# A second-layer transformer trunk kernel: one more product of the feed-forward stage as a pair, and operands of the group computed ahead emitted later

## The chip, the cores and the metric

The kernel runs on one core of a Trainium2 chip. The metric is the device time of one execution in microseconds (us); the number given for a kernel is the median of several runs. The profiles come from one further execution each, whose own time differs a little from the median.

## The reference

Two layers of a hybrid block on 512 positions of width 1024, all in 32-bit floats. A layer has a branch of matrix memory (mLSTM), a branch of retention, their gated merge, a feed-forward step and a gated embedding. The change is in the feed-forward step alone; in the reference it is two lines:

```python
h2 = rmsnorm(x, norm2_g[i])
x = x + jnp.square(jax.nn.relu(h2 @ w_ff1[i] + b_ff1[i])) @ w_ff2[i] + b_ff2[i]
```

`w_ff1[i]` is 1024 by 4096 and `w_ff2[i]` 4096 by 1024.

## The kernel before

**Products.** Activations lie transposed: 128 partitions of a feature tile by 512 positions. Each 32-bit factor is split in a high and a low part that TensorE takes at full rate: ACT copies the high part (L326), VectorE subtracts it from the source for the low part (L327). A product is then three matmuls: high by high, high by low, low by high. There are two forms for a group of two output tiles:

- two **T8** units (`t8`, matmuls at L518 to L520): per unit one weight tile of 128 by 1024 and 24 matmuls of 512 columns;
- one **PAIR** unit (`run_pair`, matmuls at L573 to L575): a scheme of Strassen and Winograd with seven products P1, P5, P6, P2, P3, P7, P4 of 12 matmuls of 256 columns each. P4 is put off: it is kept in `later` and issued by `flush`, behind P5 of the next unit (or in the middle of the next T8).

A pair takes its weights in the pieces A (for P1, P5), B (P6, P2), C (P3, P7), each 128 by 1024, and D (P4), 128 by 512. Half of each of A, B and C, and all of D, are sums of weight blocks (`t1` to `t4`). POOL makes them ahead in DRAM with accumulating DMAs (`step`, L384), one at a time, paced by a credit that grows with each unit by a share of its time: `SHARE`, and `LATER` from some unit on. Each step also waits for the matmul that was the last one issued when it was written. SP loads the pieces (`fill_raws`) into four raw buffers; three buffers hold split pieces A, B and C (and whole tiles of T8), one holds D. So a split piece waits on ACT until an older piece has been used, and a low part on VectorE for its high part on ACT.

**The feed-forward stage.** The 4096 inner features are four groups b of four parts p. `f(b,p)` computes a part of the first product with `ff1` and keeps it as an operand of the second; `o(b,p)` is a pair of the second product, adding group b's share to two tiles of x with `ff2`. The order is written out in `ff_order`: f(0,0) to f(0,3); then for b = 0, 1, 2: f(b+1,0), o(b,0) to o(b,3), f(b+1,1) to f(b+1,3); then o(3,0) to o(3,3). So f(b+1,0) is computed ahead, before group b is added up. `FPAIRS` lists for each layer which (b,p) of the first product are pairs; the others are two T8.

In `ff1`, `evac` takes each half out of PSUM: VectorE multiplies by the norm's factor (L1535), ACT does relu (L1536) and the square (L1537). From the result `st` two helpers make the operand that a pair needs, in seven quarters of 256 columns: `pair_quarters` splits the first three (a 768-column split on ACT and VectorE), and `pair_operand` forms the four inner ones on VectorE (L668, L669, L670) and splits them (a 1024-column split). The parts are `hid[b, p]`, in the trace `l0hh` and `l0hl` (or `l1hh`, `l1hl`), with five buffers each; `st` has two buffers (`l0f20st` is that of f(2,0) in layer 0).

In `ff2` each of the seven products is added onto x by VectorE as soon as it is done: L1573, or L1571 the first time, when the bias is added too. The products share three PSUM banks per pair, named in the trace by a letter behind the unit's name (`l1o11a` is bank a of o(1,1) in layer 1): P1, P6, P7 and P4 use a, P5 and P3 use c, and P2 uses b. P2 adds onto a copy of P1 that ACT puts into b (L579). So P7 can only begin when P6 has been added to x, and P3 when P5 has. Evictions are given a higher priority (`ahead`) in the scheduler that settles the order of each engine's queue; each engine then works through its queue in that order, and a row that waits holds up all behind it.

Of the kernel before, what the change touches and what calls it, by code (L numbers as in the profile page):

```python
# [87 lines left out]

FPAIRS = (((1, 1), (1, 3), (2, 1), (2, 3), (3, 1)), ((0, 2), (1, 0), (1, 1), (1, 3), (2, 0), (2, 1), (2, 3), (3, 0), (3, 1), (3, 2)))


PRODUCTS = {"P1": ("A", 0, 0), "P5": ("A", 1, 4), "P2": ("B", 0, 2), "P6": ("B", 1, 5), "P3": ("C", 0, 6),
# [14 lines left out]
HALVES = [(WIDE[x][0], u) for x, u in TURNS]  # L109

SOON = ("w_in", 0, CGM + 2 * P)
STEP, SHARE, LATER = 1.13, 0.75, 0.75
TIME = {"PAIR": (9.9, 3.9), "WIDE": (5.45, 2.7), "FULL": (9.9, 5.0)}


# [37 lines left out]
def groups():  # L153
# [3 lines left out]
    for i in range(L):  # L157
# [11 lines left out]
        for b in range(4):  # L169
            f = [p for c, p in FPAIRS[i] if c == b]  # L170
            if f:
# [5 lines left out]
def unit_list(i):  # L177
# [10 lines left out]
    def pair(g, p):  # L188
        u.append(("PAIR", (i, g), p))
# [51 lines left out]
    def pairs(seq):  # L241
        for kind, b, p in seq:
            if (b, p) in FPAIRS[i] and kind == "f":
                pair(f"fp{b}", [q for c, q in FPAIRS[i] if c == b].index(p))
            elif kind == "f":
# [13 lines left out]
def build(ctx, tc, ins, out):  # L259
# [65 lines left out]
    def split(src, hi_ap, lo_ap):  # L325
        a = ac.activation(hi_ap, src, AF.Copy)  # L326
        return a, ve.tensor_sub(lo_ap, src, hi_ap.bitcast(F32))  # L327
# [194 lines left out]
    def t8(act, name):  # L522

        _, wh, wl = unit("T8")
        o = ps(name)
        for k in range(KT):
            s = slice(k * P, (k + 1) * P)
            mm3(o, wh[:, s], wl[:, s], act[0][k], act[1][k], k == 0, k == KT - 1)
            if k == 3:
                flush()  # L530
            if k in (2, 5):
                pace()
        return o
# [100 lines left out]
    def pair_tiles(name, act, consume, y=None, then=None):  # L634

        y = y or [tmp(f"{name}y{d}") for d in range(2)]
        a, b = slice(0, S), slice(S, T)

        def done(x, o):
            with ahead():  # L640
                evict(x, o)
            if then and x in then:
                then[x]()
            if x == "P4":
                consume(y)

        def evict(x, o):
            if x == "P1" or x == "P2" and cur["own"] == "written":
                ac.activation(y[0][:, b], o, AF.Copy)
            elif x == "P5":  # L650
                ac.activation(y[1][:, a], o, AF.Copy)
            elif x == "P2":
                ve.tensor_tensor(y[0][:, b], o, y[0][:, b], OP.add)
            elif x == "P6":
                ac.activation(y[1][:, b], o, AF.Copy)
            elif x == "P3":
                ve.tensor_tensor(y[1][:, b], o, y[1][:, b], OP.add)
            elif x == "P7":
                ve.tensor_tensor(y[1][:, a], o, y[1][:, a], OP.add)
            else:  # L660
                ac.activation(y[0][:, a], o, AF.Copy)

        run_pair(name, act, done)

    def pair_operand(name, st, hi, lo):

        v = st.rearrange("p (q t) -> p q t", t=S)
        ve.tensor_tensor(v[:, 4:6, :], v[:, 1:3, :], v[:, 0:1, :].to_broadcast([P, 2, S]), OP.subtract)  # L668
        ve.scalar_tensor_tensor(v[:, 6, :], v[:, 5, :], -1.0, v[:, 1, :], OP.mult, OP.subtract)  # L669
        ve.scalar_tensor_tensor(v[:, 7, :], v[:, 6, :], -1.0, v[:, 3, :], OP.mult, OP.subtract)  # L670
        split(st[:, 4 * S:8 * S], hi[:, 3 * S:7 * S], lo[:, 3 * S:7 * S])

    def pair_quarters(st, hi, lo):
        split(st[:, S:4 * S], hi[:, 0:3 * S], lo[:, 0:3 * S])
# [131 lines left out]
    def bcol(i, n, k):  # L806
        o, _ = _B[n]
        return bvec(i, o + k)
# [216 lines left out]
    for i in range(L):  # L1025
# [38 lines left out]
        for k in range(KT):  # L1064
            s = slice(k * P, (k + 1) * P)
            f, e = k == 0, k == KT - 1
# [455 lines left out]
        cur["ff"] = cur["tmp"] = phase(f"ff{i}", ph_side)  # L1522
        cur["ntmp"] = 2
        cur["own"] = "new"
        hid = {}

        def ff1(b, p):

            nm = f"l{i}f{b}{p}"
            hid[b, p] = [cur["ff"].tile([P, 7 * S], F32R, name=f"l{i}h{a}{b}{p}", tag=f"h{a}", bufs=5) for a in "hl"]  # L1530
            st = cur["ff"].tile([P, 8 * S], F32, name=nm + "st", tag="st", bufs=2)

            def evac(d, o, sign=1.0):
                a = st[:, d * T:(d + 1) * T]
                ve.tensor_tensor(a, o, n2.b, OP.mult)  # L1535
                ac.activation(a, a, AF.Relu, bias=bcol(i, "bf1", 8 * b + 2 * p + d), scale=sign)  # L1536
                ac.activation(a, a, AF.Square)  # L1537

            if (b, p) in FPAIRS[i]:
                def consume(y):  # L1540
                    for d in range(2):
                        evac(d, y[d], SIGN[d])
                    pair_quarters(st, *hid[b, p])
                    pair_operand(nm, st, *hid[b, p])

                pair_tiles(nm, n2_seven, consume, [st[:, d * T:(d + 1) * T] for d in range(2)])
                return
            o = t8(n2.act, f"{nm}0")
            if b == 0 and p == 0:
                n2.finish()  # L1550
                o1 = t8(n2.act, f"{nm}1")
                n2.spread()
                evac(0, o)
                evac(1, o1)
            else:
                evac(0, o)
                evac(1, t8(n2.act, f"{nm}1"))
            pair_quarters(st, *hid[b, p])
            pair_operand(nm, st, *hid[b, p])

        def tile3(c):
            n3.tile(c, x[c])

        def ff2(b, p):
            started = set()

            def add(q, o, op):
                y = x[2 * p + q // 2][:, (q % 2) * S:(q % 2 + 1) * S]
                if b == 0 and q not in started:
                    started.add(q)  # L1570
                    ve.scalar_tensor_tensor(y, y, bcol(i, "bf2", 2 * p + q // 2), o, OP.add, op)  # L1571
                else:
                    ve.tensor_tensor(y, y, o, op)  # L1573

            def done(x_, o):
                if x_ in ("P1", "P2"):
                    add(1, o, OP.add)
                elif x_ == "P5":
                    add(2, o, OP.subtract)
                elif x_ in ("P6", "P3"):  # L1580
                    add(3, o, OP.subtract)
                elif x_ == "P7":
                    add(2, o, OP.subtract)
                elif x_ == "P4":
                    add(0, o, OP.add)
                    if b == 3 and p == 3:
                        tile3(6)
                        tile3(7)
                if b == 3 and p and x_ in ("P6", "P7"):
                    tile3(2 * p - 2 + (x_ == "P7"))  # L1590

            def parts(k):
                h, l = hid[b, k]
                return lambda j: (h[:, j * S:(j + 1) * S], l[:, j * S:(j + 1) * S])

            run_pair(f"l{i}o{b}{p}", [parts(k) for k in range(4)], done)

        first, rest = ff_order()
        for kind, b, p in first:
            if kind == "o":  # L1600
                ff2(b, p)
                continue
            if (b, p) == (3, 1):
                pth, ptl = [cur["ff"].tile([P, 2, T], F32R, name=f"l{i}pt{a}", tag=f"h{a}", bufs=5) for a in "hl"]
                for k in range(2):
                    t = tmp(f"l{i}ptr{k}")
                    nc.scalar.dma_start(t, ins["pT"][i, k])
                    split(t, pth[:, k, :], ptl[:, k, :])
            ff1(b, p)
# [20 lines left out]
        for _, b, p in rest:  # L1630
            ff2(b, p)
# [222 lines left out]
```

## Time and profile before

| what | before |
|---|---|
| median of 3 runs, us | 2275.59 (2275.17 to 2277.27) |
| the profiled execution's own time, us | 2276.45 |
| its span, us | 2274.7 |
| granted TensorE clock, mean | 0.999 |
| L327, low part of a piece A, mean ns | 1223 |
| L326, high part of a piece A, mean ns | 1054 |
| sums into s30t on POOL (L384), 24 steps, mean ns | 702 |
| loads of pair pieces, `wr<-wpairs`, us from issue to landing | 4.3 |

The profile page gives the busy time of each engine, the chain of work that ended last and the costliest groups of instructions; a timeline lists one engine's instructions with start, duration, name and the idle time before. PE is TensorE's matmul, PEld its weight load, DVE VectorE, ACT ScalarE, POOL GpSimd, SP the engine that issues most loads. Matmuls overlap: the time that counts is from one start to the next, not the duration.

### The profile page before, as it was taken

The page shows a single profiled execution, that of the slowest core. Times are in us where ns is not written, and L with a number is a line of the kernel's source. Part 1 is how long each engine was busy: PE and PEld are TensorE (multiplying, and loading weights), DVE is VectorE, ACT ScalarE, POOL GpSimd, SP SyncE. Part 2 cuts the span into 40 slices and gives each one's busy share as a digit, 9 for nine tenths or more (in the row PEclk, how much of TensorE's full clock was granted, in tenths as well). Part 3 has the DMA queues.
Part 4 walks back from the last instruction along what each step waited for, and adds up shares of the span by engine and source line. Part 5 has one row for each costly group of instructions (what it writes and reads, how often), then busy time and mean ns, then how long its engine had stood idle before and what let it go on. Part 6 is the DMA issues. An engine that isn't in the chain of part 4 may idle for free.

```text
span 2274.7 us, 36420 instructions
## 1 busy us (share of the span) xinstructions
PE 2262.0 (99%) x13532; PEld 2009.3 (88%) x13532; DVE 1746.7 (77%) x2680; ACT 1281.7 (56%) x1881; POOL 610.1 (27%) x952
## 2 busy tenths in 40 slices
PE   9999999999999999999999999999999999999998
PEld 8888899888898899999888888998888988999997
DVE  7877777887676877787778787678867678887786
ACT  6766544554554556556557565455545545676564
POOL 3332222223124322223442322221231243111112
PEclk9999999999999999999999999999999999999999
DMA  6776887787879888888887667877877898888851
GB/s 214 185 195 178 244 225 225 218 233 214 245 220 275 216 230 223 251 242 220 228 218 198 183 180 240 238 214 217 239 220 218 251 267 209 262 238 229 247 169 60
DMA packets 185890, 499.33 MB, mean 220 GB/s; under 512 B 26400, under 2 KB 26784, under 8 KB 185712
## 3 DMA queue, kind: packets, MB, share of 16 engines
q0 software_dynamic: 57520, 188.53, 37.4%
q1 hardware_dynamic: 112496, 280.57, 36.5%
q10 hardware_dynamic: 15696, 27.91, 3.6%
q8 instruction: 106, 1.74, 0.3%
q14 instruction: 72, 0.59, 0.1%
HBM read 478.03 MB, written 194.51 MB: 296 GB/s over the span
## 4 chain that ended last, share of the span: by engine, by line
PE 89%; DVE 4%; issue 3%; DMA 2%; ACT 2%; POOL 1%; SPq 0%; DVEq 0%; POOLq 0%; ACTq 0%
PE l0f L518 2%; PE l0f L519 2%; PE l0f L520 2%; PE l0br L518 1%; PE l1br L518 1%; PE l1br L519 1%; PE l0br L519 1%; PE l0br L520 1%; PE l1br L520 1%; PE l1f L518 1%; PE l1f L519 1%; PE l1f L520 1%; PE l0pg L518 1%; PE l0bm L518 1%; PE l0pg L520 1%
## 5 line engine op out<-in xcount | busy, mean ns | idle before, releaser
L327 DVE TENSOR_TENSOR w<-wr,w 128x1024 fp32r<-128x1024 f32 (+1 forms) x193 | 234.1, 1216 | 47.3 <-ACT w L326 45.2
L326 ACT ACTIVATE w<-wr 128x1024 fp32r<-128x1024 f32 (+1 forms) x193 | 199.7, 1041 | 122.8 <-issue 28.5
L326 ACT ACTIVATE w_B<-wr 128x1024 fp32r<-128x1024 f32 x123 | 130.2, 1059 | 128.8 <-PE l0bm L520 13.1
L327 DVE TENSOR_TENSOR w_B<-wr,w_B 128x1024 fp32r<-128x1024 f32 x123 | 151.7, 1235 | 52.8 <-ACT w_B L326 52.5
L326 ACT ACTIVATE w_C<-wr 128x1024 fp32r<-128x1024 f32 x75 | 79.7, 1062 | 88.3 <-DMA wr<-wpairs 10.4
L327 DVE TENSOR_TENSOR w_C<-wr,w_C 128x1024 fp32r<-128x1024 f32 x75 | 91.7, 1223 | 27.2 <-ACT w_C L326 23.3
L327 DVE TENSOR_TENSOR w_A<-wr,w_A 128x1024 fp32r<-128x1024 f32 x75 | 91.7, 1223 | 15.3 <-ACT w_A L326 14.9
L326 ACT ACTIVATE w_A<-wr 128x1024 fp32r<-128x1024 f32 x75 | 79.0, 1054 | 40.2 <-PE l1bm L520 4.4
L326 ACT ACTIVATE w_t<-wr 128x1024 fp32r<-128x1024 f32 x56 | 59.4, 1061 | 67.0 <-issue 7.8
L327 DVE TENSOR_TENSOR w_t<-wr,w_t 128x1024 fp32r<-128x1024 f32 x56 | 68.5, 1223 | 22.2 <-ACT w_t L326 21.3
L326 ACT ACTIVATE w_D<-wr 128x512 fp32r<-128x512 f32 x75 | 47.2, 630 | 60.1 <-issue 6.8
L518 PE MATMUL l0f<-l0n2h,w 128*128 128x512 f32 x176 | 68.7, 390 | 0.0
L519 PE MATMUL l0f<-l0n2l,w 128*128 128x512 f32 x176 | 68.6, 390 | 0.0
L520 PE MATMUL l0f<-l0n2h,w 128*128 128x512 f32 x176 | 68.5, 389 | 0.0
L327 DVE TENSOR_TENSOR w_D<-wr,w_D 128x512 fp32r<-128x512 f32 x75 | 51.7, 689 | 13.4 <-ACT w_D L326 12.8
L384 POOL DMA_DIRECT2D s30t<-wpairs x24 | 16.8, 702 | 89.4 <-PE l1o20a L575 8.8
L520 PEld LDWEIGHTS l0f<-l0n2h,w 128*128 128x128 f32 x176 | 33.0, 188 | 7.0
L518 PEld LDWEIGHTS l0f<-l0n2h,w 128*128 128x128 f32 x176 | 33.0, 188 | 6.6
L519 PEld LDWEIGHTS l0f<-l0n2l,w 128*128 128x128 f32 x176 | 33.0, 188 | 6.4
L518 PE MATMUL l1f<-l1n2h,w 128*128 128x512 f32 x96 | 37.6, 391 | 0.0
L519 PE MATMUL l1f<-l1n2l,w 128*128 128x512 f32 x96 | 37.4, 390 | 0.0
L520 PE MATMUL l1f<-l1n2h,w 128*128 128x512 f32 x96 | 37.4, 389 | 0.0
(5828 smaller groups left out, 9074.7 us busy)
## 6 DMA issues: line engine op xcount, KB each, us to landing
wr<-wstream SPq DMA_DIRECT2D x189, 512.0 KB, 5.1
wr<-wpairs SPq DMA_DIRECT2D x225, 256.0 KB, 4.3
wr<-wwide SPq DMA_DIRECT2D x48, 512.0 KB, 4.9
s3t<-wwide POOLq DMA_DIRECT2D x24, 256.0 KB, 4.7
s6t<-wwide POOLq DMA_DIRECT2D x24, 256.0 KB, 5.4
s18t<-wwide POOLq DMA_DIRECT2D x24, 256.0 KB, 5.2
s21t<-wwide POOLq DMA_DIRECT2D x24, 256.0 KB, 5.1
s24t<-wpairs POOLq DMA_DIRECT2D x24, 256.0 KB, 6.2
```

What stands on the lines that cost most here:

```text
L326: a = ac.activation(hi_ap, src, AF.Copy)
L327: return a, ve.tensor_sub(lo_ap, src, hi_ap.bitcast(F32))
L384: dma = gp.dma_start(piece(g, x, p, q), piece(g, MADE[x][a], p, q), max_dma_last_dim=4096, **kw)
L518: te.matmul(o, sh, mh, start=first, stop=False)
L519: te.matmul(o, sh, ml, start=False, stop=False)
L520: cur["mm"] = te.matmul(o, sl, mh, start=False, stop=last)
```

## The change

Three things. f(0,1) of the second layer becomes a pair instead of two T8. The operands of f(b+1,0), the parts computed ahead, are not formed right behind its `evac`: `operands` puts the two helpers in the list `behind`, and `ff2` takes one of them at its start for p of 1 or more, so `pair_quarters` is written at o(b,1) and `pair_operand` at o(b,2). The scheduler may still place their instructions further ahead, where an engine would be idle; the rows below show where they come to stand. And `LATER` is 0.76 in place of 0.75.

```diff
--- before.py
+++ after.py
@@ -88,7 +88,7 @@
 
 
 
-FPAIRS = (((1, 1), (1, 3), (2, 1), (2, 3), (3, 1)), ((0, 2), (1, 0), (1, 1), (1, 3), (2, 0), (2, 1), (2, 3), (3, 0), (3, 1), (3, 2)))
+FPAIRS = (((1, 1), (1, 3), (2, 1), (2, 3), (3, 1)), ((0, 1), (0, 2), (1, 0), (1, 1), (1, 3), (2, 0), (2, 1), (2, 3), (3, 0), (3, 1), (3, 2)))
 
 
 PRODUCTS = {"P1": ("A", 0, 0), "P5": ("A", 1, 4), "P2": ("B", 0, 2), "P6": ("B", 1, 5), "P3": ("C", 0, 6),
@@ -109,7 +109,7 @@
 HALVES = [(WIDE[x][0], u) for x, u in TURNS]
 
 SOON = ("w_in", 0, CGM + 2 * P)
-STEP, SHARE, LATER = 1.13, 0.75, 0.75
+STEP, SHARE, LATER = 1.13, 0.75, 0.76
 TIME = {"PAIR": (9.9, 3.9), "WIDE": (5.45, 2.7), "FULL": (9.9, 5.0)}
 
 
@@ -1522,13 +1522,21 @@
         cur["ff"] = cur["tmp"] = phase(f"ff{i}", ph_side)
         cur["ntmp"] = 2
         cur["own"] = "new"
-        hid = {}
+        hid, behind = {}, []
 
         def ff1(b, p):
 
             nm = f"l{i}f{b}{p}"
             hid[b, p] = [cur["ff"].tile([P, 7 * S], F32R, name=f"l{i}h{a}{b}{p}", tag=f"h{a}", bufs=5) for a in "hl"]
             st = cur["ff"].tile([P, 8 * S], F32, name=nm + "st", tag="st", bufs=2)
+
+            def operands():
+                two = lambda: pair_quarters(st, *hid[b, p]), lambda: pair_operand(nm, st, *hid[b, p])
+                for f in two:
+                    if b and p == 0:
+                        behind.append(f)
+                    else:
+                        f()
 
             def evac(d, o, sign=1.0):
                 a = st[:, d * T:(d + 1) * T]
@@ -1540,8 +1548,7 @@
                 def consume(y):
                     for d in range(2):
                         evac(d, y[d], SIGN[d])
-                    pair_quarters(st, *hid[b, p])
-                    pair_operand(nm, st, *hid[b, p])
+                    operands()
 
                 pair_tiles(nm, n2_seven, consume, [st[:, d * T:(d + 1) * T] for d in range(2)])
                 return
@@ -1555,14 +1562,15 @@
             else:
                 evac(0, o)
                 evac(1, t8(n2.act, f"{nm}1"))
-            pair_quarters(st, *hid[b, p])
-            pair_operand(nm, st, *hid[b, p])
+            operands()
 
         def tile3(c):
             n3.tile(c, x[c])
 
         def ff2(b, p):
             started = set()
+            if p and behind:
+                behind.pop(0)()
 
             def add(q, o, op):
                 y = x[2 * p + q // 2][:, (q % 2) * S:(q % 2 + 1) * S]
```

In layer 0, VectorE's queue at o(1,0) stood so before (w_A to w_D are weight pieces, `l0o10a` to `c` the banks of o(1,0), `l0f20st` and `l0hl` the part f(2,0) and its low operand):

```order
L327 TENSOR_TENSOR w_A<-wr_8866,w_A 128x1024
L327 TENSOR_TENSOR l0hl_8863<-l0f20st,l0hh_8862 128x768
L670 SCALAR_TENSOR_TENSOR l0f20st<-l0f20st 128x256
L1573 TENSOR_TENSOR l0x_7211<-l0x_7211,l0o10a 128x256
L1573 TENSOR_TENSOR l0x_7210<-l0x_7210,l0o10b 128x256
L1573 TENSOR_TENSOR l0x_7211<-l0x_7211,l0o10c 128x256
L327 TENSOR_TENSOR l0hl_8863<-l0f20st,l0hh_8862 128x1024
L327 TENSOR_TENSOR w_B<-wr_8928,w_B 128x1024
```

and stands so now (L1573 of before is L1581):

```order
L327 TENSOR_TENSOR w_A<-wr_8869,w_A 128x1024
L1581 TENSOR_TENSOR l0x_7212<-l0x_7212,l0o10a 128x256
L1581 TENSOR_TENSOR l0x_7211<-l0x_7211,l0o10b 128x256
L327 TENSOR_TENSOR l0hl_8866<-l0f20st,l0hh_8865 128x768
L327 TENSOR_TENSOR w_B<-wr_8931,w_B 128x1024
L1581 TENSOR_TENSOR l0x_7212<-l0x_7212,l0o10c 128x256
L500 TENSOR_TENSOR wr_8931<-wr_8931 128x512
L1581 TENSOR_TENSOR l0x_7212<-l0x_7212,l0o10a 128x256
L670 SCALAR_TENSOR_TENSOR l0f20st<-l0f20st 128x256
```

The 768-column split and L670 of f(2,0) have moved from ahead of the additions of banks a and b to behind them. For f(1,0) in o(0,0) it is alike: L668, the 768-column split and L669 go behind the addition of P5, and f(3,0) stands in o(2,0) as f(2,0) does here.

In layer 1, VectorE's queue from o(1,0) into o(1,1) stood so before (`l1o11a`, `b` and `c` are the banks of o(1,1), `l1f20st` the part f(2,0)):

```order
L327 TENSOR_TENSOR w_B<-wr_20474,w_B 128x1024
L327 TENSOR_TENSOR l1hl_20339<-l1f20st,l1hh_20338 128x768
L670 SCALAR_TENSOR_TENSOR l1f20st<-l1f20st 128x256
L1573 TENSOR_TENSOR l1x<-l1x,l1o10a 128x256
L327 TENSOR_TENSOR w_C<-wr_20496,w_C 128x1024
L327 TENSOR_TENSOR l1hl_20339<-l1f20st,l1hh_20338 128x1024
L1573 TENSOR_TENSOR l1x<-l1x,l1o11c 128x256
L1573 TENSOR_TENSOR l1x<-l1x,l1o10a 128x256
L327 TENSOR_TENSOR w_D<-wr_20543,w_D 128x512
L1573 TENSOR_TENSOR l1x<-l1x,l1o11a 128x256
L327 TENSOR_TENSOR w_A<-wr_20587,w_A 128x1024
L1573 TENSOR_TENSOR l1x<-l1x,l1o11b 128x256
```

and stands so now:

```order
L327 TENSOR_TENSOR w_B<-wr_20541,w_B 128x1024
L1581 TENSOR_TENSOR l1x<-l1x,l1o10a 128x256
L327 TENSOR_TENSOR l1hl_20406<-l1f20st,l1hh_20405 128x768
L327 TENSOR_TENSOR w_C<-wr_20563,w_C 128x1024
L669 SCALAR_TENSOR_TENSOR l1f20st<-l1f20st 128x256
L1581 TENSOR_TENSOR l1x<-l1x,l1o11c 128x256
L670 SCALAR_TENSOR_TENSOR l1f20st<-l1f20st 128x256
L1581 TENSOR_TENSOR l1x<-l1x,l1o10a 128x256
L327 TENSOR_TENSOR l1hl_20406<-l1f20st,l1hh_20405 128x1024
L327 TENSOR_TENSOR w_D<-wr_20602,w_D 128x512
L327 TENSOR_TENSOR w_A<-wr_20646,w_A 128x1024
L1581 TENSOR_TENSOR l1x<-l1x,l1o11a 128x256
```

The 768-column split, L669 and L670 of f(2,0) are behind an addition of bank a of o(1,0) that they stood ahead of, and L669 and L670 also behind piece C. The 1024-column split is behind the two additions that followed it, and pieces D and A now both stand ahead of the first addition of `l1o11a`. Rows of f(1,0) in o(0,1) and of f(3,0) in o(2,1) stand in the same way.

## The prediction

> **What bounds the kernel now.** I read the page first (busy time, then the chain that ended last), then a table of windows in the two feed-forward stages, then the timelines of TensorE and VectorE around each place that the change touches.
>
> ```profile
> PE 2262.0 (99%) x13532; PEld 2009.3 (88%) x13532; DVE 1746.7 (77%) x2680; ACT 1281.7 (56%) x1881; POOL 610.1 (27%) x952
> ...
> PE 89%; DVE 4%; issue 3%; DMA 2%; ACT 2%; POOL 1%; SPq 0%; DVEq 0%; POOLq 0%; ACTq 0%
> ...
> L326 ACT ACTIVATE w_B<-wr 128x1024 fp32r<-128x1024 f32 x123 | 130.2, 1059 | 128.8 <-PE l0bm L520 13.1
> ```
>
> TensorE is busy 99% of the span and is 89% of the chain. So time moves in two ways only: other matmul work, or gaps in its stream. A busy share of 99% hides small gaps, so I take the step from one matmul's start to the next one's.
>
> ```profile
> 1901.58 0.40 PE L518 MATMUL l1f<-l1n2h,w 128*128 128x512 f32 x1
> ...
> 1912.49 0.28 PE L573 MATMUL l1f02a<-l1n2h,w_A 128*128 128x256 f32 x1
> ...
> 1920.67 0.40 PE L518 MATMUL l1f<-l1n2h,w 128*128 128x512 f32 x1
> ```
>
> The 48 wide matmuls of f(0,1) in layer 1 take 1901.58 to 1912.49, 10.91 us or 227 ns each. The pair behind it does six products of 12 from 1912.49 to 1920.67: 8.18 us for 72 matmuls, 113.6 ns each. Per column the two are equal, and seven products of 12 cost 84 × 113.6 = 9.54 us.
>
> There is a second, slower tempo:
>
> ```profile
> core 0: us, PE busy (x) PEld busy (x) DVE busy (x) ACT busy (x) POOL busy (x), PEclk, DMA share, GB/s
> 821.02:861.50 40.48, 40.48 (x349) 40.48 (x348) 30.79 (x45) 17.89 (x24) 8.38 (x12) 1.00 0.88 242
> ...
> 2103.66:2156.00 52.34, 52.34 (x451) 52.34 (x450) 38.96 (x60) 31.18 (x46) 6.79 (x10) 1.00 0.88 256
> 902.00:932.00 30.00, 30.00 (x266) 30.00 (x266) 23.91 (x38) 12.71 (x17) 5.73 (x9) 1.00 0.90 262
> ```
>
> All three hold 256-column matmuls alone, at a granted clock of 1.00. From 902 a matmul takes 30.00/266 = 112.8 ns; from 821, 40.48/349 = 116.0; from 2103.66, 52.34/451 = 116.1. At the third row's pace the first would be 1.1 us shorter, the second 1.5. Nothing waits in them. Each begins just behind a gap and ends at the next longer one, or at wide matmuls.
>
> **The change part by part.** *The pair.* f(0,1) of layer 1 falls from 10.91 to 9.54 us: **−1.37**. What it adds: five SP loads (seven quarters for two whole tiles), eight sum steps on POOL, 1.5 more pieces to split and four copies and three additions of 256 columns. POOL is at 27%, and the waits of TensorE in the two stages (rows below) name no transfer. A piece costs ACT 1.06 us (the row above) and VectorE 1.22 (rows below), a small operation about 0.4, so ACT gets 1.5 × 1.06 + 4 × 0.4 = 3.2 us more and VectorE 1.5 × 1.22 + 3 × 0.4 = 3.0, in a stretch where they have this room:
>
> ```profile
> 1901.57:1912.49 10.92, 10.92 (x49) 9.01 (x48) 7.06 (x10) 7.82 (x11) 2.84 (x5) 1.00 0.81 241
> ```
>
> VectorE is idle 3.9 us there and ACT 3.1, so it fits on the whole, but that idle time lies in waits for single operations and is not all to be filled. I let ACT come 1 us late to f(1,0), a third of what is added; its P6 needs the copy at L579:
>
> ```profile
> 1934.95 0.36 ACT L579 ACTIVATE l1f10b<-l1f10a 128x256 f32<-128x256 f32 x1
> ...
> 1935.72 0.28 PE L573 MATMUL l1f10a<-l1nsh,w_B 128*128 128x256 f32 x1
> ```
>
> The copy ends at 1935.31, 0.41 us ahead of its user, so 1 us of lateness costs up to 0.6. I take +0.4 here, and +0.2 for the first product of f(0,2), whose piece A VectorE now splits behind the parts of f(0,0) and three more small operations: **+0.6** (0, all absorbed, to 1.3, both waits at double).
>
> *The later operands, layer 0.* In o(1,0) the last product P7 writes the bank that P6 used, so it waits for VectorE to add P6 to x:
>
> ```profile
> PE l0o10a L573 <- DVE l0x L1573: 0.3, 1, 0.3
> PE l0o20a L573 <- DVE l0x L1573: 0.3, 1, 0.3
> ...
> PE l0o00a L573 <- ACT l0f10st L1537: 0.2, 1, 0.2
> ...
> 898.97 1.22 DVE L327 TENSOR_TENSOR w_A<-wr,w_A 128x1024 fp32r<-128x1024 f32 x1
> 900.11 0.95 DVE L327 TENSOR_TENSOR l0hl<-l0f20st,l0hh 128x768 fp32r<-128x768 f32 x1
> 900.97 0.42 DVE L670 SCALAR_TENSOR_TENSOR l0f20st<-l0f20st 128x256 f32<-128x256 f32 x1
> 901.31 0.41 DVE L1573 TENSOR_TENSOR l0x<-l0x,l0o10a 128x256 f32<-128x256 f32 x1
> ...
> 901.25 0.28 PE L573 MATMUL l0o11a<-l0hh,w_A 128*128 128x256 f32 x1
> 901.78 0.39 PE L573 MATMUL l0o10a<-l0hh,w_C 128*128 128x256 f32 x1 [0.26 <-DVE l0x L1573]
> 902.00 0.28 PE L574 MATMUL l0o10a<-l0hl,w_C 128*128 128x256 f32 x1
> ```
>
> The steps 901.25 to 901.78 to 902.00 are 0.75 us where two normal ones are 0.23: 0.52 lost, and the same in o(2,0). The 768-column split and L670 stood ahead of the addition; now they stand behind it. It starts when w_A's split lets it, at 900.11, and is done at 900.52, 0.84 us ahead of P7. Both gaps go: **−1.0**. The operands themselves are used first by o(2,0), behind o(1,1) to o(1,3) and f(2,1) to f(2,3); they have time, and what counts is only where they now stand. In layer 0 no addition falls behind them that TensorE then needs at once.
>
> In o(0,0) the same move concerns the addition of P5, for which P3 waits:
>
> ```profile
> 817.71 0.96 DVE L327 TENSOR_TENSOR l0hl<-l0f10st,l0hh 128x768 fp32r<-128x768 f32 x1
> ...
> 818.92 0.48 DVE L1571 SCALAR_TENSOR_TENSOR l0x<-l0x,bc,l0o00c 128x256 f32<-128x256 f32 x1
> ...
> 819.56 0.34 PE L573 MATMUL l0o00c<-l0hh,w_C 128*128 128x256 f32 x1
> 819.74 0.28 PE L574 MATMUL l0o00c<-l0hl,w_C 128*128 128x256 f32 x1
> ```
>
> The addition ends at 819.40, P3 begins at 819.56 with a step of 0.18, and the slow tempo runs from 821 to 861.5. L668, the split and L669, which stood between w_D's split and the addition, move behind it: it can start at 817.7 where the split did, 1.2 us earlier. If this small gap starts the slow tempo, that goes: **−1.1** (0 to −1.2). I take it whole, as that gap is the nearest one ahead of the window.
>
> *The later operands, layer 1.* There f(b+1,0) is a pair, its inner parts are done later still, and the gap they make is elsewhere:
>
> ```profile
> 1952.03 1.22 DVE L327 TENSOR_TENSOR w_B<-wr,w_B 128x1024 fp32r<-128x1024 f32 x1
> 1953.17 0.42 DVE L1573 TENSOR_TENSOR l1x<-l1x,l1o00a 128x256 f32<-128x256 f32 x1
> ...
> 1953.29 0.28 PE L575 MATMUL l1o01c<-l1hh,w_A 128*128 128x256 f32 x1
> 1953.64 0.38 PE L573 MATMUL l1o00a<-l1hh,w_D 128*128 128x256 f32 x1
> 1953.86 0.28 PE L574 MATMUL l1o00a<-l1hl,w_D 128*128 128x256 f32 x1
> ```
>
> P4 waits here for the addition of P7: 0.57 us for two steps, 0.34 lost. The 768-column split and L670 leave its front, so **−0.34**. But they now reach the next unit. Before, in o(1,1) (and likewise in o(0,1) and o(2,1)):
>
> ```profile
> 2031.15 0.42 DVE L670 SCALAR_TENSOR_TENSOR l1f20st<-l1f20st 128x256 f32<-128x256 f32 x1
> ...
> 2032.95 1.22 DVE L327 TENSOR_TENSOR l1hl<-l1f20st,l1hh 128x1024 fp32r<-128x1024 f32 x1
> ...
> 2034.75 0.69 DVE L327 TENSOR_TENSOR w_D<-wr,w_D 128x512 fp32r<-128x512 f32 x1
> 2035.36 0.42 DVE L1573 TENSOR_TENSOR l1x<-l1x,l1o11a 128x256 f32<-128x256 f32 x1
> 2035.69 1.22 DVE L327 TENSOR_TENSOR w_A<-wr,w_A 128x1024 fp32r<-128x1024 f32 x1
> ...
> 2037.55 0.28 PE L573 MATMUL l1o11a<-l1hh,w_C 128*128 128x256 f32 x1
> ```
>
> P6's addition had ended at 2035.78, 1.8 us ahead of P7. Now the 1024-column split stands right ahead of w_D, and w_A too stands ahead of the addition. That split needs L670, then ACT's half (1.05 us). L670 ended at 2031.57; it gets w_C's split (1.22, of which neighbours overlap about 0.08) and two additions (0.33 each) ahead of it that stood behind, so it ends at 2033.4, ACT's half at 2034.6, the split at 2035.8, w_D's at 2036.4, w_A's at 2037.6, and the addition at 2038.0: P7 comes 0.45 late. The rows stand alike in o(0,1) and o(2,1), and I take the same there: **+1.35**. If VectorE only had w_A's split more ahead and never waited for ACT, the addition would end at 2036.9 and cost nothing, so 0 to 1.6.
>
> The gaps at o(1,0) and o(2,0) stay: they wait for a split of f(1,3) and f(2,3), which is not moved.
>
> ```profile
> PE l1o10c L574 <- DVE l1hl L327: 0.4, 1, 0.4
> PE l1o20c L574 <- DVE l1hl L327: 0.4, 1, 0.4
> ```
>
> *The share 0.76.* It issues sum steps somewhat earlier. No wait of TensorE on these sums appears in the two stages, so 0 (−0.1 to +0.2).
>
> *Sum.* −1.37 + 0.6 − 1.0 − 1.1 − 0.34 + 1.35 = **−1.9 us**. The profiled execution took 2276.45 (span 2274.7), so it would take 2274.6. It lies 0.9 above the median of 2275.59 of three runs, so the forecast for the median is **2273.7**.
>
> **A rule of the skill that speaks against the pair.** The Trainium skill, TensorE: Matmul & The Clock Gate, section "Back-to-back issue gap", states sustained spacings of about 81 ns at 128 columns and 131 ns at 512; halfway by columns this gives an estimate of 98 ns at 256. By that page 84 small matmuls would take 8.2 us and 48 wide ones 6.3, and the pair would cost 1.9 us instead of gaining 1.37. The rows above (227 and 113.6 ns) do not agree with it, and the mechanism it would need is the fourth rival.
>
> **The rivals.**
>
> *All gains, no new gaps* (2270.3). ACT's order leaves layer 1's additions in time, the 0.6 of the pair isn't paid, and the slow tempo from 2103.66 does not begin: −1.37 − 1.0 − 1.1 − 0.34 − 1.5 = −5.3, so 2270.3. For it: VectorE is busy 77%, and the slow tempo from 2103.66 begins just behind o(2,0)'s wait of 0.4, of which o(1,0) has an equal one, so it does not look bound to come. Against: the count for o(1,1).
>
> *The pair alone counts* (2274.9). The slow tempo in layer 0 was started by an earlier gap that stays (its P6 waits 0.2 for ACT at L1537, row above), and layer 1 takes back (+1.0) what o(1,0) and o(2,0) of layer 0 give: −1.37 + 0.6 − 1.0 + 1.0 = −0.7.
>
> *Slower: the moved splits hold up layer 1's P7.* Place: the additions of o(0,1), o(1,1), o(2,1). It decides against the change from the point where such an addition ends after P7 is due (2037.55 in o(1,1), by rows of before), and a short gap there starts the slow tempo, as the step of 0.18 at 819.56 may have. Each then costs 0.45 and some 300 matmuls × 3.2 ns = 1.0 us: 3 × 1.45 = +4.3, with the pair's +0.6 and layer 0's tempo unchanged: −1.37 + 0.6 − 1.0 − 0.34 + 4.3 = +2.2, so 2277.8.
>
> *Slower: short matmuls held by their weight loads.* If all 84 ran at the slow tempo's 116.1 ns the pair would still take 9.75 and gain 1.16; it loses from 10.91/84 = 130 ns on, which no window here shows. Late transfers for the pair would do the same: a load stalled by 4 us or more, with the DMA share at 0.81 in the window of f(0,1), would bring +5 us or 2280.6. I see no wait for a load there.
>
> **How the numbers follow.** Forecast 0.45 (its own range 2272.5 to 2275.0), all gains 0.13, pair alone 0.23, P7 held up 0.15, matmuls or transfers slow 0.04. The range 2270.3 to 2277.0 takes the forecast, the pair alone, half of all gains and the lower third of P7 held up. About 0.2% (4.6 us) is what a measurement of this kernel can tell from no change; by that, faster means below 2271.0 and slower above 2280.1. Faster: nearly all of the first rival, 0.12. Slower: the last rival, 0.04. The rest, 0.84, is the same within the bound.
>
> **What would show it.** From the first matmul of f(0,1) to that of f(0,2) in layer 1 it should be 8.2 us, six products, with P4 behind the first two of f(0,2). The steps ahead of P7 in o(1,0) and o(2,0) of layer 0 should be 0.11; the window of 349 matmuls behind 821 should run at 113 ns, not 116. In layer 1, P7 of o(0,1), o(1,1), o(2,1) should show a gap of 0.4 to 0.5 that was not there, and P4 of o(0,0) none. The forecast is wrong if a slow window appears behind one of these, if that from 2103.66 is gone, or if TensorE waits for a DMA between 1880 and 1945.

## The result and the profile after

| kernel | us, median | against before, with its 95% interval |
|---|---|---|
| before | 2277.06 (2273.89 to 2280.02, 16 runs) | |
| changed | 2280.24 (2277.19 to 2283.96, 16 runs) | 1.0019 (1.0012 to 1.0025) |

The change makes the kernel slower by 0.19%, 4.3 us by the ratio, where 1.9 us less was forecast. The profiled execution took 2278.47 us (span 2276.4), 2.0 more than that of before, so it shows half of the loss.

First the changed kernel's page (busy time, share and instructions of each engine), then TensorE's waits in the second layer's feed-forward stage and in its mLSTM (who waited for whom, us in total, times, longest):

```profile
PE 2260.8 (99%) x13568; PEld 2008.9 (88%) x13568; DVE 1749.2 (77%) x2684; ACT 1282.7 (56%) x1888; POOL 614.9 (27%) x960
...
PE l1o01a L573 <- DVE l1x L1579: 1.7, 1, 1.7
PE l1o00a L573 <- DVE l1x L1579: 0.5, 1, 0.5
PE l1o11a L573 <- DVE l1x L1581: 0.5, 1, 0.5
PE l1o10c L574 <- DVE l1hl L327: 0.4, 1, 0.4
PE l1o20c L574 <- DVE l1hl L327: 0.3, 1, 0.3
PE l1f10a L573 <- ACT l1f10b L579: 0.3, 1, 0.3
...
PE l1m0ot L905 <- DVE l1m0num L899: 0.8, 1, 0.8
PE l1m0s L520 <- DVE l1m0kl L327: 0.4, 1, 0.4
```

TensorE is busy 1.2 us less than before, with 36 matmuls more, and six products of f(0,1) take 8.40 us from its first matmul to that of f(0,2), where 8.2 was forecast: the pair itself works. What is new are the waits. Those at `l1o10c` and `l1o20c` were there before; four at P6 and P7 of the second layer's feed-forward stage are new; the two last, new too, lie 700 us earlier, in the second layer's mLSTM, where neither the pair nor the operands reach. There the queues of TensorE, VectorE, ACT and SP hold the same rows in the same order as before; only the sums on POOL, which the share paces, stand differently.

The first layer does what was forecast at o(1,0) and o(2,0). In TensorE's timeline of the changed kernel P7 of o(1,0) is followed by o(1,1) at the normal step:

```profile
900.46 0.28 PE L575 MATMUL l0o10a<-l0hh,w_C 128*128 128x256 f32 x1
900.58 0.28 PE L573 MATMUL l0o11a<-l0hh,w_A 128*128 128x256 f32 x1
```

0.12 us, and the like in o(2,0). One wait there was not forecast: P7 of the first layer's o(0,1) begins 0.37 us late by the steps, for the addition of P6. In the second layer the addition for which P7 of o(0,1) waits is late. VectorE, ACT and TensorE of the changed kernel, start and duration first:

```profile
1955.33 0.42 DVE L670 SCALAR_TENSOR_TENSOR l1f10st<-l1f10st 128x256 f32<-128x256 f32 x1
1955.66 0.48 DVE L1579 SCALAR_TENSOR_TENSOR l1x<-l1x,bc,l1o00a 128x256 f32<-128x256 f32 x1
1956.87 1.23 DVE L327 TENSOR_TENSOR l1hl<-l1f10st,l1hh 128x1024 fp32r<-128x1024 f32 x1 [0.73 <-ACT l1hh L326]
1958.01 0.69 DVE L327 TENSOR_TENSOR w_D<-wr,w_D 128x512 fp32r<-128x512 f32 x1
1958.62 1.22 DVE L327 TENSOR_TENSOR w_A<-wr,w_A 128x1024 fp32r<-128x1024 f32 x1
1959.75 0.47 DVE L1579 SCALAR_TENSOR_TENSOR l1x<-l1x,bc,l1o01a 128x256 f32<-128x256 f32 x1
...
1955.78 1.06 ACT L326 ACTIVATE l1hh<-l1f10st 128x1024 fp32r<-128x1024 f32 x1 [3.10 <-DVE l1f10st L670]
...
1958.35 0.28 PE L575 MATMUL l1o01c<-l1hh,w_C 128*128 128x256 f32 x1
1960.28 0.39 PE L573 MATMUL l1o01a<-l1hh,w_C 128*128 128x256 f32 x1 [1.65 <-DVE l1x L1579]
```

That is the chain of the prediction's third rival: L670 late, ACT's half behind it, VectorE idle 0.73 us for it, then the split, w_D, w_A and only then the addition.

And in the mLSTM VectorE waits for the writing of two gate tiles to DRAM (`gm_spill`). The first row is of before, the two others of the changed kernel; in the bracket stands the idle time ahead:

```profile
1213.56 0.29 DVE L1121 TENSOR_SCALAR l1m0D<-l1m0rb,l1gct 128x128 f32<-128x128 f32 x1 [0.34 <-DMA gm_spill<-l1bgm0g]
```

```profile
1212.86 0.29 DVE L1121 TENSOR_SCALAR l1m0D<-l1m0rb,l1gct 128x128 f32<-128x128 f32 x1 [2.00 <-DMA gm_spill<-l1bgm0g]
1216.19 0.42 DVE L871 TENSOR_TENSOR l1m0p<-l1m0s,l1m0D 128x256 f32<-128x256 f32 x1 [1.35 <-DMA gm_spill<-l1bgm1g]
```

0.34 us before, 3.35 now. The steps of the sums that POOL issues beside it differ: before, four accumulating ones begin between 1205 and 1213; now five others begin between 1202.6 and 1210.

### The profile page after: what moved, and what is told of

Its sections match the earlier page's. It is cut to its first block, busy times and chain, and to the rows that moved or that the text cites. A ratio compares the mean times of both kernels' runs of the same rounds, so it can differ in the third digit from the quotient of the medians.

```text
span 2276.4 us, 36525 instructions
## 1 busy us (share of the span) xinstructions
PE 2260.8 (99%) x13568; PEld 2008.9 (88%) x13568; DVE 1749.2 (77%) x2684; ACT 1282.7 (56%) x1888; POOL 614.9 (27%) x960
## 5 line engine op out<-in xcount | busy, mean ns | idle before, releaser
L500 DVE TENSOR_TENSOR wr<-wr 128x512 f32<-128x512 f32 x49 | 33.7, 687 | 0.5
L384 POOL DMA_DIRECT2D s6t<-wwide x24 | 17.1, 711 | 61.1 <-PE l0g0va L626 20.5
L384 POOL DMA_DIRECT2D s24t<-wpairs x24 | 16.8, 701 | 58.6 <-PE l1g0va L626 12.0
```

Of the source, the lines that this page charges most:

```text
L384: dma = gp.dma_start(piece(g, x, p, q), piece(g, MADE[x][a], p, q), max_dma_last_dim=4096, **kw)
L500: ve.tensor_tensor(r[:, :Q], r[:, :Q], r[:, Q:], OP.add)
```

## The experiments

The theories: **A**, the moved operands cost the time, in the second layer. **B**, the share 0.76 costs it, by sums that meet the writing of the gate tiles to DRAM (the spills). **C**, the spill wait only differs between executions. **D**, the share costs in many places. **E** and **F** are about why the pair brings so little: **E**, two pairs one behind the other leave ACT and VectorE late; **F**, a pair at f(0,1) is bad in itself. Each run was timed in five rounds against the kernel before on the same chip: e1 to e4, e5 to e8, e9 to e12 and e13 to e16 share the runs of before.

| run | pairs | share | operands later in | against before |
|---|---|---|---|---|
| e1 | 10 | 0.76 | none | 1.0020 (1.0008 to 1.0032) |
| e12, e1 again | 10 | 0.76 | none | 1.0021 (1.0011 to 1.0030) |
| e5 | 10 | 0.76, then 0.75 | none | 1.0006 (0.9998 to 1.0015) |
| e14, e5 again | 10 | 0.76, then 0.75 | none | 1.0011 (1.0001 to 1.0022) |
| e13 | 10 | 0.75, then 0.76 | none | 1.0011 (0.9998 to 1.0024) |
| e2 | 11 | 0.76 | none | 1.0012 (1.0003 to 1.0020) |
| e6 | 11 | 0.75, then 0.78 | none | 1.0013 (1.0004 to 1.0022) |
| e9 | 10, (0,1) for (0,2) | 0.75 | none | 0.9999 (0.9991 to 1.0008) |
| e10 | 11, (0,3) for (0,1) | 0.76 | none | 1.0004 (0.9995 to 1.0012) |
| e3 | 10 | 0.75 | both layers | 1.0001 (0.9993 to 1.0010) |
| e11 | 10 | 0.75 | layer 0 | 0.9987 (0.9978 to 0.9995) |
| e16, e11 again | 10 | 0.75 | layer 0 | 0.9999 (0.9990 to 1.0008) |
| e4, the change again | 11 | 0.76 | both layers | 1.0015 (1.0007 to 1.0024) |
| e7 | 11 | 0.75, then 0.78 | both layers | 1.0010 (1.0002 to 1.0019) |
| e15 | 11 | 0.76 | layer 0 | 1.0013 (1.0003 to 1.0022) |
| e8 | 11 | 0.75, then 0.78 | layer 0 | 1.0006 (0.9997 to 1.0015) |

"Then" is the first retention unit of the second layer, behind the spills. The pair could not be tried with 0.75 throughout: its sums are then not all issued when its pieces are loaded.

**The parts apart (e1 to e4).** e1 is the share alone, in the kernel of before:

```diff
-STEP, SHARE, LATER = 1.13, 0.75, 0.75
+STEP, SHARE, LATER = 1.13, 0.75, 0.76
```

> Only LATER 0.76, FPAIRS and the operands as before. Theory A (the moved operands in layer 1 cost the time: P7 of o(0,0), o(0,1), o(1,1) wait 0.74, 1.93 and 0.74 us in the profile after): within 1 us of before. Theory B (sums issued earlier meet the spills of the gates in layer 1's mLSTM; VectorE then waits 3.4 us for them between 1207 and 1217 instead of 0.3): +2 to +3 us, and that wait shows in the profile. Theory C (that wait differs between executions whatever the share): no steady difference.

1.0020: the share alone costs as much as the whole change. VectorE waited 2.94 us at the spills. So a loss of this size needs no moved operands, and A is not the whole cause; e1 doesn't show how much A costs inside the change. e2 adds (0, 1) to the second layer's `FPAIRS`:

> f(0,1) as a pair and LATER 0.76, the operands as before. Theory A: faster than before by 0.5 to 1.4 us (the pair's 1.37 less 0.5 at P6 of f(1,0)). Theory B: +1 to +2 us. The P7 waits of 1.93 and 0.74 us in layer 1 absent by A and B both; if they are there, the pair made them and not the moved operands.

1.0012. On one chip with e1 this is 0.08% less, within both intervals, so the pair neither gained nor lost clearly. Its price is in the profile of e2, in TensorE's waits:

```profile
PE l1f10a L573 <- ACT l1f10b L579: 1.4, 1, 1.4
PE l1o00a L573 <- DVE l1x L1573: 0.6, 1, 0.6
```

No wait at P7 of o(0,1), o(1,1) or o(2,1) is there; those belong to the operands. e3 is `operands` and `behind` alone:

> Only the operands of f(b+1,0) later; ten pairs and LATER 0.75 as before. Theory A: layer 0 gains 2 to 3 us, layer 1 loses 2.5 to 3.5: 0 to +1.5 us. Theory B: layer 1 as in A and no wait at the spills: 0 to +1.5 too, so with e1 it tells the sizes apart. My forecast of 0.45 each at three places would give -1.2.

1.0001. The profile of e3 has the P7 waits without the pair, and no wait at f(1,0):

```profile
PE l1o21a L573 <- DVE l1x L1581: 0.8, 1, 0.8
PE l1o01a L573 <- DVE l1x L1579: 0.6, 1, 0.6
```

As steps from one matmul to the next it loses 0.89, 0.42 and 1.05 us at the three places, 2.4 in all, and the first layer's two gaps, 1.0 together, are gone. By these rows it should be about 1 us slower; the interval can't tell that from nothing. e4:

> The changed kernel beside the three others on one chip: +3 to +5 us against before. If the parts add, it is e2 plus e3 less what they share.

1.0015, so the first result holds.

**Where the share costs, and the change with the share moved (e5 to e8, e13, e14).** e5 and e14, with `branch` the index of the first retention unit of the second layer:

```diff
-        at["credit"] += (SHARE if at["unit"] <= rush else LATER) * t - load
+        at["credit"] += (SHARE if at["unit"] <= rush else 0.76 if at["unit"] <= branch else LATER) * t - load
```

> LATER 0.76 only up to the first retention unit of the second layer (so over the second layer's mLSTM), 0.75 behind it; ten pairs and the operands as before. Theory B (the earlier sums meet the gate spills at 1204 to 1217 and hold VectorE): +1.5 to +3 us, VectorE's wait for the spills 1.5 us or more. Theory D (the share costs in many small places, or at the end, where P4 of o(3,3) waits 0.64 us in e1): +0.5 or less.

> e5 a second time, beside e13 on one chip. If the two parts add to the 0.2% of e1 and e12, e13 and e14 together come to +4 to +5 us; if only the early part counts, this one is +3 to +5 and e5 was a low draw.

e13 is the reverse, 0.75 up to `branch` and 0.76 behind it:

> LATER 0.75 up to the first retention unit of the second layer, 0.76 behind it; ten pairs, operands as before. If the share costs over the second layer's mLSTM alone (spills): within 1 us of before, and VectorE waits under 0.5 us for the spills. If it costs by what it shifts behind that (waits at P4 of o(0,0) and of o(3,3), the retention's w_D): +2 to +4.

1.0006 and 1.0011 for the early part, 1.0011 for the late one; the intervals of e5 and e13 include no change. The two halves are compatible with half of the 0.2% each; which counts more isn't settled. What the share does at the spills is settled. The table has VectorE's idle time there, summed over both rows (0 where no such wait is listed), and the time that TensorE takes from the first matmul of `l1m0s` to the first of `l1m2z`, the stretch of the mLSTM around them, in the eighteen profiles:

| share over the second layer's mLSTM | VectorE's wait at the spills, us | TensorE's stretch, us |
|---|---|---|
| 0.76: after, e1, e2, e4, e5, e10, e12, e14, e15 | 3.35, 2.94, 1.56, 0.23, 1.73, 3.10, 1.13, 1.05, 3.52 | 53.25, 52.37, 51.14, 51.20, 52.11, 52.35, 51.17, 51.03, 52.55 |
| 0.75: before, e3, e6, e7, e8, e9, e11, e13, e16 | 0.34, 0, 0, 0.28, 0, 0.40, 0, 0, 0 | 50.57, 50.56, 50.57, 50.57, 50.56, 50.57, 50.56, 50.57, 50.57 |

So C falls. With 0.75 the stretch is the same to 0.01 us in nine of nine; with 0.76 it is longer in nine of nine, by 0.5 to 2.7 us, though the size differs between executions (the changed kernel has 2.68 and, as e4, 0.63). The spills are not all of it: e4 loses its 0.63 with a wait there of 0.23. And it is not all that the share costs: 1.3 us on the mean, where e1 and e12 are some 4.6 us slower in time.

In e1, e5, e12 and e14 the second layer's retention, from the first matmul of `l1bm` to that of `l1wo`, is longer too: 431.5 to 433.1 us, against 430.6 to 431.4 in the nine profiles with 0.75. In the five with 0.76 and eleven pairs it is not, 430.7 to 430.9. So the share costs the kernel of ten pairs something that it doesn't cost the change, and its 0.2% can't be carried over whole. e6 takes the pair with the share raised behind the spills only (0.78 from there):

> f(0,1) as a pair, LATER 0.75 up to the first retention unit of the second layer and 0.78 behind it, which is enough for the pair's sums; the operands as before. Theory B: no wait for the spills beyond 0.5 us, and 1 to 3 us less than e2 in time, so -1.4 to +1 against before. Theory D: as e2, +2 to +4. By both P6 of f(1,0) waits 0.5 to 1.7 us for ACT, which leaves little of the pair's 1.37.

1.0013 and no wait at the spills, but 0.9 us at P6 of f(1,0). Without the meeting at the spills the pair is no better than with it, though 0.78 behind them may cost something of its own, which no run has alone. e7 and e8 put the operands on top, e8 with `if i == 0 and b and p == 0` in `operands`:

> The whole change, but with the share raised only behind the second layer's mLSTM (0.75, then 0.78). Theory B: 2 to 4 us faster than the change, about -1 to +1 against before. Theory A (the moved operands' waits at P7 of the second layer, 2.3 to 2.9 us in two profiles): still slower than before by 1 to 3.

> As e7, with the operands later in the first layer only. P7 of o(0,1), o(1,1), o(2,1) in the second layer should show no wait, and the gaps at P7 of o(1,0) and o(2,0) in the first layer none either. By A and B the fastest so far: -1 to -4 us against before.

1.0010 and 1.0006: neither beats before. Against e4 (1.0015) e7 is no clear gain either, so inside the change the times don't show what the share costs; only the profiles do. In the profile of e8 P4 of o(0,0) alone waits 2.4 us for VectorE, and then TensorE runs at a lower granted clock (the figure ahead of the DMA share):

```profile
1953.00:1957.00 4.00, 3.65 (x18) 3.65 (x19) 3.46 (x6) 1.12 (x4) 0.00 (x0) 0.57 0.54 151
```

Fourteen steps behind the wait take 0.213 us each in place of 0.113, 1.4 us more.

**Why the pair brings nothing (e9, e10).** e9 swaps which part is the pair, at the same number of sums and loads:

```diff
-((0, 2), (1, 0), (1, 1), (1, 3), (2, 0), (2, 1), (2, 3), (3, 0), (3, 1), (3, 2))
+((0, 1), (1, 0), (1, 1), (1, 3), (2, 0), (2, 1), (2, 3), (3, 0), (3, 1), (3, 2))
```

> f(0,1) a pair instead of f(0,2), so again ten pairs; LATER 0.75 and the operands as before: as many matmuls, sums and loads as before. Theory E (the pair loses because two pairs in a row, f(0,1) and f(0,2), leave ACT late at f(1,0)): P6 of f(1,0) waits 0.3 us or less, P4 of o(0,0) no longer than before (0.34), time within 1 us of before. Theory F (a pair at f(0,1) is bad in itself, by its pieces being made in the norm's stretch): the waits of 0.5 to 1.7 us are there and it is 1 to 3 us slower.

0.9999, and in the list of e9's waits in that stage only the two at o(1,0) and o(2,0) that before has:

```profile
PE l1o10c L574 <- DVE l1hl L327: 0.4, 1, 0.4
PE l1o20c L574 <- DVE l1hl L327: 0.4, 1, 0.4
```

So a pair at f(0,1) is not bad in itself (F falls), and e1, with 0.76 and ten pairs, has no wait at f(1,0) either: it takes f(0,1) and f(0,2) both. e10 puts the eleventh pair at (0,3) in place of (0,1), with 0.76:

> Eleven pairs with f(0,3) in place of f(0,1), LATER 0.76, operands as before. Now f(0,2), f(0,3) and f(1,0) are pairs without a unit of wide matmuls between them. Theory E: waits at P6 or P4 of f(1,0) and o(0,0) as large as in e2 or larger, time +2 to +5. Theory F: no waits of that size at f(1,0), -1 to +1.

The waits of e10 are now at o(0,0), for its piece A:

```profile
PE l1o00a L575 <- DVE w_A L327: 0.8, 1, 0.8
PE l1o00a L573 <- ACT w_A L326: 0.7, 1, 0.7
```

1.9 us by the steps, for the same gain of matmul time. Here too the granted clock is lower behind them, and 15 steps of about 0.213 us add 1.5 us:

```profile
1943.00:1946.00 3.00, 3.00 (x16) 3.00 (x16) 3.00 (x4) 2.02 (x3) 0.05 (x1) 0.50 0.64 184
```

In no other of the eighteen profiles does the clock fall in these stages, not in e7 with its wait of 1.9 us either. By the waits E stands: two pairs in succession ahead of f(1,0) leave ACT and VectorE behind, and the next unit that needs them at once pays. By the time it is not confirmed: E asked for +2 to +5 us, and 1.0004, with the share at 0.76 throughout, is the least of all runs with that share. What makes up for the waits is open.

**The operands in the first layer alone (e11, e16), and in the change (e15).** e11 and e16 have `if i == 0 and b and p == 0` and nothing else of the change:

> The operands later in the first layer only, ten pairs, LATER 0.75. The gaps at P7 of o(1,0) and o(2,0) go (0.5 us each), nothing changes in the second layer: -0.5 to -2 us, which five rounds may not resolve. If the moved operands were a loss in the first layer too, it would be above before.

> e11 a second time: again 1 to 4 us faster than before, if it was no draw; by the two gaps alone, 1.

0.9987, then 0.9999. The gaps at P7 of o(1,0) and o(2,0) are gone in both profiles, but the time of the first did not come again, so these two times don't show a gain. One difference between them is the wait at P7 of o(0,1), which e11 does not have; it costs e16 1.02 us by the steps:

```profile
PE l0o01a L573 <- DVE l0x L1579: 0.7, 1, 0.7
```

Over all profiles the first layer's part does show. From the first matmul of its o(0,0) to the first of the stage behind its feed-forward (`l0pe`) the eight with the operands moved there take 228.0 to 230.6 us, 229.2 on the mean, and the ten without 229.2 to 233.9, 231.6 on the mean. Of the 2.4 us between the means, 0.8 is gaps and 1.5 the tempo of the matmuls (below). This comparison was not planned, and each profile is a single execution. e12 and e15:

> e1 a second time. Theory B: again +2 to +5 us, with VectorE's wait for the gate spills above 1 us and a wait at P4 of o(3,3) in the profile. If e1 was a draw of the spread between executions: within 1.5 us of before.

> The change with its later operands in the first layer only (pair and 0.76 stay). By e3 and e11 the second layer's part costs 0.1%: 1 to 3 us faster than the change, so +0.5 to +3 against before. If it is as slow as the change, the second layer's part costs nothing beside the pair's own waits.

e12 again gives 1.0021. e15 at 1.0013 lies between e4 (1.0015) and no difference, too near to either to price the second layer's operands inside the change.

## Why the prediction was wrong, point by point

- **The share 0.76 at 0 (−0.1 to +0.2).** This step failed, and by most. It rested on TensorE's waits in the two feed-forward stages, where no sum or load appeared. But the share sets the sums from a unit of the first layer on, so it also moves them against everything in the second layer's mLSTM and retention, which no step looked at. Two runs give it alone 0.2%, some 4.6 us, in the kernel of ten pairs. In the change's own profiles TensorE's stretch at the spills is 2.7 and 0.6 us longer; what more it costs the change is open. The sign stood in the trace of before: VectorE waited 0.34 us for a spill. The prediction spoke of no rival in which the share cost anything.
- **Slower by moved splits at P7 (0.15).** The mechanism was right, and I took it as a term of the sum too. Its size was off: +1.35 in the prediction, and by steps 1.93 + 0.74 + 0.23 = 2.9 us in the profile after, 2.4 in e3 and 2.3 in e4. After has a wait at P7 of o(0,0) too, 0.74 us, that was not foreseen. What the sum missed, as far as the rows tell: the pair had already made ACT and VectorE late when they came to o(0,1), where 1.93 was lost against 0.89 in e3 without it. But e4, the same kernel, lost 0.80 there, so the size differs between executions.
- **The gaps of the first layer, −1.0.** Right: both are gone in every profile with the operands moved there. But "in layer 0 no addition falls behind them that TensorE then needs at once" was wrong: P7 of o(0,1) is late by 0.37 us after, 0.82 in e8 and 1.02 in e16, and by less than 0.1 in the five others.
- **The pair, −1.37 + 0.6.** The matmul time is gained. The waits it makes were put at 0.6 (0 to 1.3); P6 of f(1,0) alone lost 0.54 us after, 1.66 in e2, 1.18 in e6 and 1.27 in e4, and P4 or P7 of o(0,0) more. The range was too narrow, because late ACT was carried to one user only. The fourth rival did not come about: 72 of its matmuls took 8.40 us, waits included. (The 98 ns estimated there for 256 columns lie a third of the way from 128 to 512, not halfway; they enter no sum.)
- **The slow tempo, −1.1.** Wrong in its reason. I put it down to the small gap at 819.56. The gap is gone after and the tempo with it, but e1 has that gap and the faster tempo, and e12, which is e1 again, has no step above 0.13 us there and a tempo slower still. A window inside that stretch, for before, the changed kernel, e1 and e12 in this order (length, then busy time and number of TensorE's matmuls, then its weight loads):

```profile
832.00:858.00 26.00, 26.00 (x225) 26.00 (x224) 18.52 (x29) 11.70 (x16) 6.00 (x9) 1.00 0.83 230
```

```profile
832.00:858.00 26.00, 26.00 (x231) 26.00 (x231) 18.55 (x27) 12.04 (x18) 6.10 (x10) 1.00 0.88 260
```

```profile
832.00:858.00 26.00, 26.00 (x232) 26.00 (x231) 18.64 (x28) 11.91 (x18) 6.29 (x10) 1.00 0.88 257
```

```profile
832.00:858.00 26.00, 26.00 (x219) 26.00 (x218) 17.77 (x28) 11.40 (x16) 6.12 (x10) 1.00 0.85 238
```

As steps between starts the four run at 116.7, 113.3, 113.3 and 120.0 ns on the mean. So the tempo differs between executions of one kernel (e1 and e12, on two chips; and the changed kernel ran at 116.7 as e4). Still it goes with the operands: of the eight profiles with the first layer's moved, five run at 113.3 here and three at 116.7; of the ten without, three at 113.3, one at 116.7 and six at 120.0. With the 1.5 us of tempo above, the size of the term came out about right on the mean, by luck as far as the reason goes; why is not shown.

- **The range and the chances.** The time lies outside the range, on the slower side: 4.3 us more instead of 1.9 less by the ratio. The chances had 0.15 for P7 held up and 0.04 for the rest of the slower side; slower by less than 0.2% was counted as same, and a measured 1.0019 is at that edge.

## What to carry to other kernels

A number that paces background transfers moves them against every later stage, so its cost is looked for in all of them, not only in the stage that it was raised for; here it showed where VectorE waits for another DMA. TensorE's list of waits shows no transfer as long as the present pace happens to miss them; VectorE's 0.34 us of before was the only sign. And saved matmul time counts only if the engines that feed and empty it have room in that same stretch: a busy share of ACT of 70% over a window (7.82 of 10.92 us) hid that it is late where two dense units follow one another.

## What the runs showed of the hardware that had not been expected

Executions of one kernel differ by several us, and the tempo of the 256-column matmuls can be most of it. I counted, over each whole profile, the steps between starts of such matmuls from 114.5 to 130 ns, each by what it has above 113.3 ns, and apart from them the longer gaps (for 512 columns those above 240 ns, by what they have above 226.7). e1 and e12 are one kernel; their spans are 2275.3 and 2280.9 us. The tempo gives 4.8 and 10.4 us, the gaps 16.3 and 16.6. So 5.5 of the 5.6 us of difference are tempo, at a granted clock of 0.999 in both. It is not always so: e11 and e16, one kernel too, differ by 2.9 us, of which the gaps have 2.6 and the tempo 1.0.

Four profiles with the share raised early and no eleventh pair (e1, e5, e12, e14) have on the mean 2.3 us more gaps and 2.5 us more tempo than six with 0.75 there (before, e3, e9, e11, e13, e16): together 4.8 us, about the 0.2% that the share costs in time. That the share makes the tempo slower is not shown by this: the four have 4.8 to 10.4 us of it, the six 3.9 to 7.7, and three of the six have the first layer's operands moved. What starts the slower tempo was not found: all eighteen profiles have the same step of 0.43 us at P6 of the first layer's o(0,0), and either tempo follows it.
